# A gated delta rule's z products and gates, moved from behind the four groups into each group

## The chip, the cores and the metric

The kernel runs on one core of a Trainium2 chip, in one launch. The metric is device microseconds of one execution. Three runs of the kernel before took 2798.03, 2798.21 and 2803.38 us; the median is 2798.21.

The engines are named as in the profile: PE is TensorE (matmul and transpose; PEld its weight loads), DVE is VectorE, ACT is ScalarE, POOL is GpSimd, SP is SyncE, which issues nearly all DMA transfers.

## The reference

Two blocks of two layers over 512 positions of width 1024, in float32. The change touches one mixer of the second block, the gated delta rule:

```
proj = x @ w_in                         # q, k, v, z of 8 heads x 128, and gates
q, k, v = silu(conv4(q, k, v))          # then q, k normalised per head
# per head, in chunks: A = strict_lower((beta k) k^T * decay); solve (I + A) u = beta v
for chunk n:                            # state S: 128 x 128 per head
    v_new = u_n - w_n S
    o_n   = (q_n * exp(gc)) S + (q k^T * decay) v_new
    S     = S * d_n + k_dec^T v_new
o = rms_norm(o, norm_w) * silu(z)       # z: the gate of the output
return o @ w_o                          # here gdn_wo
```

Behind it come residual, layer norm and a mixture of 16 experts, then a second layer.

## The kernel before

Every product with weights is done three times with float32r halves (`mm3`: high x high, high x low, low x high). A piece of weights, 128 x 1024, is loaded by SP (`ws<-in_...`, 512 KB), its high half copied out on ACT (L130), its low half formed on DVE (L131); `ws` has 4 buffers, the halves 3 each.

`gdn` (L786) works on four groups of two heads. `gdn_group` (L894) does in program order:
- products of k, q and v (`lin_f`, six pieces of gdn_w, 24 matmuls of 128x512 each), convolution and silu on DVE and ACT, transposes to token order (L917);
- decay and k q^T for four chunks of 128 positions, giving B and Q (L973 to L985);
- the inverse of I + A on its 16x16 diagonal blocks: B is stored to DRAM (L998), the diagonal blocks are loaded as W (L999), solved on DVE in small steps (L1002 to L1028), stored (L1029) and loaded back as X (L1030);
- transposes of X (L1034) and three levels that widen the inverse to 32, 64 and 128 (L1036 to L1069): matmuls L1055, L1062, L1065, then L1044 and L1049, each level with DVE steps between;
- the scan over the four chunks (L1075 to L1120), which leaves the output `ot` and its sums of squares; then the root (`rsqrt`, 12 small DVE steps).

Behind all four groups come the products of z (`lin_t`, L872): for each group two pieces of gdn_wz and, for four token tiles, 24 matmuls of 128x256; each result goes through tanh on ACT (L869) and one DVE step (L870) into `sz`. Then, per head, four gates on DVE (L884), four transposes (L885), a scaled copy on ACT (L886) and its low half on DVE (L887) give `ys`. `out_moe` (L1125) multiplies `ys` with gdn_wo in products of 24 matmuls; a product needs all eight heads, k by k.

Buffers are rings named by a tag: x has 16 buffers of 128 x 1024 (the input `xs` holds 8 until the last product with it, a group holds KQ twice, ktok and vtok), h has 4 (`ot`). In PSUM, `lin` has 2 banks, `s` 3, `o` 2, `pt` 1.

The code gives a program order. The order in each engine's queue is fixed when the program is built: instructions are taken in program order, but one whose inputs or buffer are not ready yet (by the builder's own reckoning) is overtaken by later ones that are. On the chip each queue then runs strictly in that order.

Of the kernel before, what the change touches and what calls it, by code (L numbers as in the profile page):

```python
# [11 lines left out]
AF = mybir.ActivationFunctionType  # L12
OP = mybir.AluOpType
# [7 lines left out]
NT = 4  # L21
# [8 lines left out]
def rd(ap):  # L30
    return ap.bitcast(F32)


class Kern:
# [751 lines left out]
    def gdn(self):  # L786
        nc, xs = self.nc, self.xs
# [6 lines left out]
        def ev_ab(o, p):  # L794
# [9 lines left out]
        a, e, u, v = (self.small((128, 2 * U), x) for x in ("a", "e", "u", "v"))  # L804
# [14 lines left out]
                                       op0=OP.mult, op1=OP.mult)  # L819
# [34 lines left out]
        for x in self.xdram:  # L854
            nc.sync.dma_start(x[:1024].rearrange("(p n) c -> p (n c)", p=128), zero)
            nc.sync.dma_start(x[1024:], zero[:8, :128])
        ot = []
        for grp in range(4):
            ot.append(self.gdn_group(grp))
            self.strips_skew(grp)  # L860
        hr = self.small((128, NT), "hr")
        nc.vector.tensor_scalar(hr, self.rcol, 0.5, None, op0=OP.mult)
        sz = []

        def ev_z(c, t, p):
            if t == 0:
                sz.append(self.T("sz", "x").rearrange("p (n i c) -> p n i c", n=NT, i=2))
            th, z = self.t("zt", tag="P")[:, :256], sz[c].rearrange("p n i c -> p n (i c)")[:, t]
            nc.scalar.activation(th, p, AF.Tanh, scale=hr[:, t:t + 1])  # L869
            nc.vector.scalar_tensor_tensor(z, th, 1.0, p, op0=OP.add, op1=OP.mult)  # L870

        self.lin_t(self.wap("gdn_wz", 8, 256), range(4), xs, ev_z)  # L872
        ys = self.ys = [self.rpair("gy") for _ in range(8)]
        for grp in range(4):
            o, rs = ot[grp]
            nc.vector.tensor_tensor(rs.rearrange("p (n i) -> p n i", i=2), rs.rearrange("p (n i) -> p n i", i=2),
                                    self.rcol[:, :, None].to_broadcast([128, NT, 2]), op=OP.mult)
            for i in range(2):
                h = 2 * grp + i
                p = self.psum("o")  # L880
                for n in range(NT):
                    u = 2 * n + i
                    ou = o[:, u * 128:(u + 1) * 128]
                    nc.vector.scalar_tensor_tensor(ou, ou, rs[:, u:u + 1], sz[grp][:, n, i], op0=OP.mult, op1=OP.mult)  # L884
                    nc.tensor.transpose(p[:, n * 128:(n + 1) * 128], ou, self.ident)  # L885
                nc.scalar.activation(ys[h][0], p, AF.Copy, scale=nw)  # L886
                nc.vector.scalar_tensor_tensor(ys[h][1], p, nw, rd(ys[h][0]), op0=OP.mult, op1=OP.subtract)  # L887
        self.dump_ys("d_gy", self.ys)
# [5 lines left out]
    def gdn_group(self, grp):  # L894
        nc, xs, wv, lvl = self.nc, self.xs, self.gconv, self.lvl
# [26 lines left out]
        ss = self.small((128, 16), "ss", tag="gA", bufs=3)  # L922
# [27 lines left out]
        g16 = lambda x: x.rearrange("p (n i) -> p n i", i=2)  # L950
# [22 lines left out]
        for n in range(NT):  # L973
# [4 lines left out]
            for i in range(2):  # L978
                u = 2 * n + i
# [11 lines left out]
        ublk = lambda x, u: x[:, u * 128:(u + 1) * 128]  # L991
# [36 lines left out]
            product(V, (0, 1), V, (0, 0), W, (1, 0))  # L1028
        nc.sync.dma_start(diag(xd), rc(V))  # L1029
        nc.sync.dma_start(v8(X), full(xd))  # L1030
        for hf in range(2):
            p = self.psum("s")
            for j in range(4):
                nc.tensor.transpose(p[:, j * 128:(j + 1) * 128], ublk(X, 4 * hf + j), self.ident)  # L1034
            self.copy(Y[:, hf * S:(hf + 1) * S], p)
# [36 lines left out]
        ot = self.T("ot", "h")  # L1072
        ss = self.small((128, 8), "oss", tag="gss", bufs=4)
# [45 lines left out]
            if n < NT - 1:  # L1119
                Sp = Sn  # L1120
        nc.vector.tensor_scalar(ss, ss, 1.0 / 128, 1e-6, op0=OP.mult, op1=OP.add)
        return ot, self.rsqrt(ss, 8)


    def out_moe(self, wname, ys, layer, out=None):  # L1125
# [917 lines left out]
```

## Time and profile before

| | |
|---|---|
| median of the runs | 2798.21 us |
| profiled execution | 2798.65 us, span 2796.9 us |
| PE busy | 2682.8 us (96%) |
| DVE busy | 1770.3 us (63%) |
| ACT busy | 1367.6 us (49%) |
| POOL busy | 181.9 us (7%) |
| DMA | 332.58 MB, mean 119 GB/s |
| mean granted clock of TensorE | 0.982 |

The delta rule lies between about 1505 and 1850 us of the span. Busy shares are averages over stages with different limits; the rows below show this stage by itself.

### The profile page before, as it was taken

The numbers are of one execution on the slowest core, as the hardware profiler recorded it, in microseconds if no ns is written. First come the engines' busy times: TensorE is split into PE (matmuls) and PEld (weight loads), VectorE is DVE, ScalarE is ACT, GpSimd is POOL, SyncE is SP. The second block draws the span as 40 slices with busy tenths as digits, with TensorE's granted clock in tenths as the row PEclk, the third lists the DMA queues.
The fourth block names the chain that finished last, engine by engine and source line by source line (L and its number), as shares of the span: only waits on it lengthen the run. The fifth ranks groups of instructions, "written<-read, shape, count | busy, mean of one in ns | idle before, by whom it ended". The sixth has DMA issues, their size and how long they took to land. (4 is left out here: it accounts for less than half of the span.)

```text
span 2796.9 us, 40163 instructions
## 1 busy us (share of the span) xinstructions
PE 2682.8 (96%) x15128; PEld 2294.2 (82%) x15128; DVE 1770.3 (63%) x3583; ACT 1367.6 (49%) x2541; POOL 181.9 (7%) x185
## 2 busy tenths in 40 slices
PE   8999999999999999999999999997997999997996
PEld 6889888888888888888887788997886888897885
DVE  6775564443447656535445877567878367667878
ACT  5654443332346544423334644335885255534885
POOL 1101010000111010100002000000001001000001
PEclk9999999999999999999999999998999999998998
DMA  4314233333333331334433222323887212013985
GB/s 138 100 41 148 70 94 92 97 98 98 91 86 92 106 106 42 109 98 127 149 94 128 85 71 63 93 69 129 303 291 275 91 42 73 24 45 100 313 295 190
DMA packets 122534, 332.58 MB, mean 119 GB/s; under 512 B 21716, under 2 KB 37748, under 8 KB 122328
## 3 DMA queue, kind: packets, MB, share of 16 engines
q1 hardware_dynamic: 119896, 321.43, 36.4%
q0 software_dynamic: 2432, 8.46, 0.8%
q8 instruction: 123, 2.02, 0.3%
q14 instruction: 83, 0.68, 0.1%
HBM read 301.49 MB, written 28.02 MB: 118 GB/s over the span
## 5 line engine op out<-in xcount | busy, mean ns | idle before, releaser
L130 ACT ACTIVATE wh<-ws 128x1024 fp32r<-128x1024 f32 (+2 forms) x521 | 534.1, 1030 | 828.8 <-PE lin L153 594.8
L131 DVE TENSOR_TENSOR wl<-ws,wh 128x1024 fp32r<-128x1024 f32 (+2 forms) x521 | 616.6, 1192 | 154.8 <-ACT wh L130 152.5
L152 PE MATMUL lin<-xs,wh 128*128 128x512 f32 (+2 forms) x1080 | 428.3, 397 | 7.4 <-ACT xs L197 5.9
L153 PE MATMUL lin<-xs,wh 128*128 128x512 f32 (+2 forms) x1080 | 429.0, 397 | 2.6 <-DVE xs L198 2.4
L154 PE MATMUL lin<-xs,wl 128*128 128x512 f32 (+2 forms) x1080 | 427.7, 396 | 0.9 <-DVE wl L131 0.9
L152 PEld LDWEIGHTS lin<-xs,wh 128*128 128x128 f32 (+2 forms) x1080 | 202.9, 188 | 50.9 <-ACT xs L197 6.8
L153 PEld LDWEIGHTS lin<-xs,wh 128*128 128x128 f32 (+2 forms) x1080 | 203.0, 188 | 47.6 <-DVE xs L198 7.1
L154 PEld LDWEIGHTS lin<-xs,wl 128*128 128x128 f32 (+2 forms) x1080 | 203.0, 188 | 42.3 <-DVE wl L131 1.4
L347 DVE TENSOR_TENSOR h<-lin,h 128x512 f32<-128x512 f32 x112 | 77.4, 691 | 247.6 <-PE lin L154 247.5
L152 PE MATMUL lin<-sr,wh 128*128 128x512 f32 x512 | 199.2, 389 | 0.0
L153 PE MATMUL lin<-sr,wh 128*128 128x512 f32 x512 | 199.2, 389 | 0.0
L154 PE MATMUL lin<-sr,wl 128*128 128x512 f32 x512 | 199.2, 389 | 0.0
L734 DVE SCALAR_TENSOR_TENSOR ra<-lin,bc 128x512 f32<-128x512 f32 x64 | 44.3, 692 | 168.5 <-PE lin L154 165.9
L305 ACT ACTIVATE P<-s,mn 128x256 f32<-128x256 f32 (+1 forms) x224 | 114.3, 514 | 52.7 <-DVE mn L303 50.1
L1539 PE MATMUL o<-oh,Rh 128*128 128x256 f32 x512 | 131.1, 292 | 5.6 <-PEq L1382 2.2
L1539 PE MATMUL o<-oh,Rl 128*128 128x256 f32 x512 | 130.0, 290 | 0.0
L152 PEld LDWEIGHTS lin<-sr,wh 128*128 128x128 f32 x512 | 96.1, 188 | 20.1
L154 PEld LDWEIGHTS lin<-sr,wl 128*128 128x128 f32 x512 | 96.1, 188 | 19.9
L153 PEld LDWEIGHTS lin<-sr,wh 128*128 128x128 f32 x512 | 96.1, 188 | 19.8
L153 PE MATMUL s<-wl,exh 128*128 128x512 f32 x256 | 105.1, 410 | 5.3 <-DVE wl L131 5.1
L313 PE MATMUL o<-c_ident,P 128*128 128x128 f32 x536 | 97.0, 282 | 12.2 <-ACT P L305 11.4
L1539 PEld LDWEIGHTS o<-oh,Rh 128*128 128x128 f32 x512 | 101.7, 199 | 8.6 <-ACT ex L1555 4.1
(605 smaller groups left out, 6174.4 us busy)
## 6 DMA issues: line engine op xcount, KB each, us to landing
ws<-in_moe_wgu SPq DMA_DIRECT2D x128, 512.0 KB, 5.9
ws<-in_mlp_wu SPq DMA_DIRECT2D x64, 512.0 KB, 3.6
ws<-in_mlp_wd SPq DMA_DIRECT2D x64, 512.0 KB, 3.6
ws<-in_moe_wd SPq DMA_DIRECT2D x64, 512.0 KB, 5.6
yd<-ey SPq DMA_DIRECT2D x56, 256.0 KB, 4.7
ws<-in_gdn_w SPq DMA_DIRECT2D x24, 512.0 KB, 3.7
ws<-in_ab_w SPq DMA_DIRECT2D x16, 512.0 KB, 4.4
ws<-in_xa_wk SPq DMA_DIRECT2D x16, 512.0 KB, 3.7
```

Of the source, the lines that this page charges most:

```text
L130: nc.scalar.activation(wh, ws, AF.Copy)
L131: nc.vector.tensor_tensor(wl, ws, rd(wh), op=OP.subtract)
L152: mm(out, a[0], b[0], start=start, stop=False)
L153: mm(out, a[0], b[1], start=False, stop=False)
L154: mm(out, a[1], b[0], start=False, stop=stop)
L305: nc.scalar.activation(P[:, :nk], p[:, :nk], AF.Exp, bias=mn, scale=-1.0, accum_out=den)
L313: nc.tensor.transpose(pt[:, b * 128:(b + 1) * 128], P[:, b * 128:(b + 1) * 128], self.ident)
L347: self.nc.vector.tensor_tensor(self.hT[n], p, self.hT[n], op=OP.add)
L734: nc.vector.scalar_tensor_tensor(a, p, 0.0, rms()[1], op0=OP.max, op1=OP.mult)
L1539: self.nc.tensor.matmul(p[:, j * 256:(j + 1) * 256], Rs[t][i][:, fs], oh[:, t], start=t + i == 0, stop=t == NT - 1 and i == 1)
```

## The change

The products of z and their evacuation move from `gdn` into `gdn_group`, behind the load of X and ahead of its transposes; each group makes only its own `sz`. The factor of the root and the eight gates of a group move to the end of `gdn_group`, which returns the gated `ot`. The half of `rcol` (`hr`) is formed ahead of the groups. What is left behind the groups is transposes, scaling and splitting. No matmul, transfer or other step is added or taken away.

```diff
+        self.hr = self.small((128, NT), "hr")
+        nc.vector.tensor_scalar(self.hr, self.rcol, 0.5, None, op0=OP.mult)
         ot = []
         for grp in range(4):
             ot.append(self.gdn_group(grp))
             self.strips_skew(grp)
-        hr = self.small((128, NT), "hr")
-        nc.vector.tensor_scalar(hr, self.rcol, 0.5, None, op0=OP.mult)
-        sz = []
-
-        def ev_z(c, t, p):
-            if t == 0:
-                sz.append(self.T("sz", "x").rearrange("p (n i c) -> p n i c", n=NT, i=2))
-            th, z = self.t("zt", tag="P")[:, :256], sz[c].rearrange("p n i c -> p n (i c)")[:, t]
-            nc.scalar.activation(th, p, AF.Tanh, scale=hr[:, t:t + 1])
-            nc.vector.scalar_tensor_tensor(z, th, 1.0, p, op0=OP.add, op1=OP.mult)
-
-        self.lin_t(self.wap("gdn_wz", 8, 256), range(4), xs, ev_z)
         ys = self.ys = [self.rpair("gy") for _ in range(8)]
         for grp in range(4):
-            o, rs = ot[grp]
-            nc.vector.tensor_tensor(rs.rearrange("p (n i) -> p n i", i=2), rs.rearrange("p (n i) -> p n i", i=2),
-                                    self.rcol[:, :, None].to_broadcast([128, NT, 2]), op=OP.mult)
             for i in range(2):
                 h = 2 * grp + i
                 p = self.psum("o")
                 for n in range(NT):
                     u = 2 * n + i
-                    ou = o[:, u * 128:(u + 1) * 128]
-                    nc.vector.scalar_tensor_tensor(ou, ou, rs[:, u:u + 1], sz[grp][:, n, i], op0=OP.mult, op1=OP.mult)
-                    nc.tensor.transpose(p[:, n * 128:(n + 1) * 128], ou, self.ident)
+                    nc.tensor.transpose(p[:, n * 128:(n + 1) * 128], ot[grp][:, u * 128:(u + 1) * 128], self.ident)
...
         nc.sync.dma_start(diag(xd), rc(V))
         nc.sync.dma_start(v8(X), full(xd))
+
+        sz = self.T("sz", "x")
+
+        def ev_z(c, t, p):
+            th, z = self.t("zt", tag="P")[:, :256], sz[:, t * 256:(t + 1) * 256]
+            nc.scalar.activation(th, p, AF.Tanh, scale=self.hr[:, t:t + 1])
+            nc.vector.scalar_tensor_tensor(z, th, 1.0, p, op0=OP.add, op1=OP.mult)
+
+        self.lin_t(self.wap("gdn_wz", 8, 256), [grp], xs, ev_z)
         for hf in range(2):
...
-        return ot, self.rsqrt(ss, 8)
+        rs = self.rsqrt(ss, 8)
+        nc.vector.tensor_tensor(g16(rs), g16(rs), self.rcol[:, :, None].to_broadcast([128, NT, 2]), op=OP.mult)
+        for u in range(8):
+            ou = ublk(ot, u)
+            nc.vector.scalar_tensor_tensor(ou, ou, rs[:, u:u + 1], ublk(sz, u), op0=OP.mult, op1=OP.mult)
+        return ot
```

## Rows read from the trace of the kernel before

**Rows 1.** Busy time by stretch (us; busy and instructions by engine, clock, DMA share, GB/s).
```profile
1573.40:1636.20 62.80, 61.95 (x385) 52.55 (x384) 46.67 (x94) 29.02 (x82) 1.84 (x2) 1.00 0.25 70
1636.20:1699.40 63.20, 60.83 (x392) 52.05 (x391) 47.75 (x114) 31.76 (x92) 1.84 (x2) 1.00 0.21 61
1699.40:1764.20 64.80, 63.42 (x422) 55.20 (x421) 49.80 (x117) 31.09 (x92) 1.84 (x2) 1.00 0.23 68
1764.20:1849.80 85.60, 81.61 (x655) 79.94 (x654) 55.27 (x155) 32.55 (x73) 0.40 (x4) 0.94 0.33 101
```
**Rows 2.** Timeline of SyncE's issues (start, us, queue, line, transfer, count).
```profile
1580.12 3.42 SPq L129 DMA_DIRECT2D ws<-in_gdn_w  x2
...
1661.80 0.33 SPq L129 DMA_DIRECT2D ws<-in_gdn_w  x1
1672.68 0.33 SPq L129 DMA_DIRECT2D ws<-in_gdn_wz  x1
...
1764.19 0.38 SPq L998 DMA_DIRECT2D b<-B  x1
```
**Rows 3.** Timeline of TensorE where the products of z begin (start, us).
```profile
1741.40 0.48 PE L154 MATMUL lin<-xs,wl 128*128 128x512 f32 x1
1741.71 0.28 PE L152 MATMUL lin<-wh,xs 128*128 128x256 f32 x1
1741.83 0.28 PE L153 MATMUL lin<-wl,xs 128*128 128x256 f32 x1
```
**Rows 4.** Busy time of line L152 alone, ahead of group 3's store (PE, PEld).
```profile
1741.60:1764.20 22.60, 3.76 (x13) 2.33 (x13) 1.00 0.08 24
```
**Rows 5.** Timeline of TensorE, first transposes and products with gdn_wo.
```profile
1836.61 1.04 PE L885 MATMUL o<-c_ident,ot 128*128 128x128 f32 x8
...
1838.86 0.39 PE L152 MATMUL lin<-wh,gy 128*128 128x256 f32 x1 [1.06 <-ACT gy L886]
...
1849.80 0.28 PE L154 MATMUL lin<-wh,gy 128*128 128x256 f32 x1
```
**Rows 6.** Timeline of TensorE, levels of groups 0 and 1 (idle before, releaser).
```profile
1601.42 1.07 PE L1034 MATMUL s<-c_ident,X 128*128 128x128 f32 x8 [0.45 <-DMA X<-x]
...
1665.41 1.09 PE L1034 MATMUL s<-c_ident,X 128*128 128x128 f32 x8 [1.83 <-DMA X<-x]
...
1667.76 0.39 PE L917 MATMUL pt<-c_ident,KQ 128*128 128x128 f32 x2
...
1687.19 0.36 PE L980 MATMUL s<-gmask,identr 128*128 128x256 f32 x1
...
1687.62 0.61 PE L1092 MATMUL o<-vtok,X 128*128 128x128 f32 x4
```
**Rows 7.** Timeline of TensorE, levels of group 3.
```profile
1787.97 1.09 PE L1034 MATMUL s<-c_ident,X 128*128 128x128 f32 x8 [2.40 <-DMA X<-x]
1790.27 3.51 PE L1055 MATMUL s<-Y,B 128*128 128x64 f32 x16
...
1800.39 2.00 PE L1055 MATMUL s<-Y,B 128*128 128x64 f32 x16
...
1812.19 0.61 PE L1092 MATMUL o<-vtok,X 128*128 128x128 f32 x4
```
**Rows 8.** Busy time by stretch of 2 us, with the granted clock.
```profile
1790.00:1792.00 2.00, 2.00 (x12) 2.00 (x11) 1.19 (x2) 0.00 (x0) 0.00 (x0) 0.50 0.19 14
...
1796.00:1798.00 2.00, 2.00 (x19) 2.00 (x19) 0.00 (x0) 0.00 (x0) 0.00 (x0) 0.96 0.56 227
```
**Rows 9.** Busy time by stretch of 10 us, the routing behind.
```profile
1910.00:1920.00 10.00, 7.53 (x38) 7.46 (x39) 6.38 (x38) 2.07 (x5) 0.00 (x0) 0.55 0.01 4
1920.00:1930.00 10.00, 5.40 (x40) 4.92 (x40) 5.66 (x24) 4.41 (x8) 0.15 (x1) 0.96 0.53 157
```
**Rows 10.** Timeline of VectorE, root and last gates of group 3.
```profile
1832.69 0.17 DVE L1121 TENSOR_SCALAR oss<-oss 128x8 f32<-128x8 f32 x1 [0.82 <-ACT jk L1118]
...
1835.53 1.67 DVE L884 SCALAR_TENSOR_TENSOR ot<-ot,b,sz 128x128 f32<-128x128 f32 x6
...
1838.69 0.62 DVE L884 SCALAR_TENSOR_TENSOR ot<-ot,b,sz 128x128 f32<-128x128 f32 x2
```
**Rows 11.** Instructions of four source lines: ns min/median/max, first and last start.
```profile
L870 DVE SCALAR_TENSOR_TENSOR sz<-zt,lin x16: 401/415/422, 1765.6 to 1838.2; 128x256 f32<-128x256 f32 x16
L884 DVE SCALAR_TENSOR_TENSOR ot<-ot,b,sz x32: 222/346/352, 1766.0 to 1839.0; 128x128 f32<-128x128 f32 x32
L886 ACT ACTIVATE gy<-o,gdn_nw x8: 678/689/692, 1838.1 to 1847.7; 128x512 fp32r<-128x512 f32 x8
L887 DVE SCALAR_TENSOR_TENSOR gy<-o,gdn_nw,gy x8: 743/749/753, 1839.2 to 1848.4; 128x512 fp32r<-128x512 f32 x8
```

## The prediction, made before the changed kernel was built or run

> **What bounds the kernel now.** I read the page's busy table first, then busy time by stretch for the delta rule, then the timelines of SyncE, TensorE and VectorE around its end. TensorE is the engine that is full: between one group's store of B and the next one's it idles 0.85, 2.37 and 1.38 us in periods of 62.8, 63.2 and 64.8 us, while VectorE has 15 to 16 us free in each [rows 1]. So in groups 0 to 2 the kernel is bound by the sum of TensorE's work, and the long chain of a group (store of B, inverse, transfer back, levels, scan) is covered by products of others.
>
> What covers it is to be seen in the order of the queues. Loads of the next group's weights stand between the store of B and the transfer back of group 0; the gate's weights are first loaded right after the last of the 24 pieces of gdn_w [rows 2], and the first product of z starts 0.31 us after the last product of group 3 [rows 3]. The order is thus the program's, except that what waits for something is overtaken by later work that is ready. Group 3 has no next group. Its cover is z: in the 22.6 us ahead of its store of B, 13 matmuls of L152, so some 39 of the 384 for z, are issued [rows 4]; the other 345 at 0.12 us each [rows 3], 41 us, lie beside group 3's chain, and TensorE is busy 81.61 of the 85.6 us from that store to the end of the first two products with gdn_wo [rows 1, 5].
>
> **The change part by part.** *The products of z.* Each group gets its own 96 matmuls (8 slices of k, 3 products, 4 token tiles), 96 x 0.12 = 11.5 us [rows 3]. They stand in program order ahead of the transposes of X and ahead of the next group's products, and their two loads of 512 KB ahead of the next group's loads. "Behind the inverses' transfer" does not hold them there: a load that is ready overtakes a waiting transfer, as those of gdn_w did [rows 2]. Total work is the same, so the question is only what each piece now covers. Groups 0 to 2 have their cover already, and the new products delay everything behind them: group 3's store of B comes 3 x 11.5 = 34.6 us later, less what falls into idle time. That idle is 0.85 + 2.37 + 1.38 = 4.6 us at most [rows 1], much of it waits for the transfer of X in an ordered queue (0.45 and 1.83 us, [rows 6]) that stay; I take 1.5 us back. Ahead of group 3's store the place of the 39 matmuls of now is taken by its own z. **First term: +33 us** (bounds +30 to +35; +40 with a bubble, the third rival).
>
> *Group 3's chain without its cover.* From the store of B to the end of the second product with gdn_wo it takes 85.6 us now [rows 1, 2, 5]. Piece by piece, now and after:
> - store to transposes of X: 1764.19 to 1787.97, 23.8 us. Mostly transfers and VectorE; the rest of group 3's z (under 60 matmuls, 7 us) lies here. 23 (21 to 24).
> - levels, to the scan's first product: 1787.97 to 1812.19, 24.2 us [rows 7]; in group 1, at full clock and with products between, 22.2 [rows 6]. Without products between, at most 2 us less; but TensorE will have stood for long. Now, after 2.4 us of waiting, the granted clock went to 0.50, its lower level of 1.2 GHz, until about 1796 [rows 7, 8], and the same 16 matmuls of L1055 took 3.51 us there and 2.00 at 2.4 GHz [rows 7]. All six such groups slow would be 9 us. In 1910 to 1920, with TensorE 75% busy, the clock was 0.55, in the next stretch 0.96 at 54% [rows 9]. So half of that: 25 (20 to 30).
> - scan: 1812.19 to 1832.69, 20.5 us [rows 7, 10]; half a us less for each of four steps without z between, some of it lost again to the clock. 20 (18 to 24).
> - root and gates: 1832.69 to 1835.53 for the root, then eight gates at 1.67 / 6 = 0.28 us [rows 10]; the eight need no longer wait for z's last tile, as the last two do now (1838.69). 5 (to 6.6 now).
> - transposes, scaling and split to the end of two products: until 1849.80 now, 10.5 us after the last gate's end at 1839.3. In the new kernel heads 0 to 5 are gated long before, so their transposes and 36 of the 48 matmuls of each pair of products are done in the chain's idle time. Left are 2.25 us from transpose to first product [rows 5], under 1 us for the second head (estimate from 0.69 and 0.75 us for a scaling and a split, [rows 11]) and 12 matmuls at 0.12: 4.5 (4 to 6).
>
> Sum 77.5 against 85.6: **second term -8 us** (-18 to +3). **Third term +1 us** (0 to +3): the remaining products with gdn_wo start at the lower clock where they now start at 1.0 or nearly.
>
> The Trainium skill, "TensorE: Matmul & The Clock Gate", section "Part 1: The HAM clock gate", has the throttled state as the default, released only by activity. By that rule alone the levels and the scan of a bare chain run slow throughout, and the sum would be about 9 us more than mine; the rows just named show both levels at such shares, and I go by them.
>
> *The gates at each group's end.* 32 gates of 0.346 us and 16 evacuations of 0.415 us on VectorE [rows 11] move forward: per group 8 x 0.35 + 4 x 0.42 = 4.4 us, and two splits of weights, into periods with 15 us free there [rows 1]. They cost nothing on the path, except behind a split that TensorE waits for; at most some 2 us a group if that cover were gone (estimate: half of it), inside the bounds. The tanh on ScalarE moves with them; hr moves as one small instruction. Zero.
>
> **Sum.** +33 - 8 + 1 = +26 us. On the profiled execution's 2798.65 us (span 2796.9) that is 2824.6; against the median of the runs, 2798.21, 2824. As a check by work: of those 77.5 us TensorE has about 38 of work, so 39 stand idle, against 4 idle and 5 lost to the clock now [rows 1]: +30, less the idle filled before.
>
> **The rivals.**
> - *The fill moves for nothing, no change.* Group 2's last k and q were transposed at 1667.76 and its decay products began only at 1687.19 [rows 6]: 20 us of slack. If that slack carries the delay of z(0) and z(1), group 3's store moves by some 20 us only, and with a chain at full clock (-18) the sum is +2: 2801. Against it: TensorE has no idle time for the displaced work to go to.
> - *The other sign: the order keeps z late.* If the products of z are held back (by a buffer of the ring, by weights) and group 3 keeps them as cover, the first two terms vanish and the gain at the end stays: 10.5 - 4.5 = 6 us, and 1.5 of idle: 2791. It decides when most of z is still undone at the last store of B. For it: z's results need a buffer that group 3's predecessors hold. Against: only two banks of PSUM take products, so a held z also stops the next group's.
> - *A bubble from buffers.* The ring x has 16 buffers; the layer's input takes 8, a group 5 instead of 4, so two groups no longer fit, and v of the next group and its z wait for the scan. At some 4 us in groups 1 to 3: +38, 2837. TensorE's idle time per period would show it.
>
> The Trainium skill, "Perfetto Trace Analysis", section "Optimization Strategy", reads a gap that repeats on the engine that should be full as a sign that buffers ran out. The trace of before shows no such gap beyond the transfer of X; the rule would lend this last rival its place.
>
> **How the numbers follow.** Forecast 0.62, no change 0.12, z kept late 0.13, bubble 0.13. The likeliest's own range is 2811 to 2843 by the ends of the terms; the range given, 2796 to 2838, leaves out most of the z-late case and the top of the bubble. Under 0.2% (5.6 us) a measurement of this kernel can't tell from none: faster 0.13, same 0.11 (most of the no-change case), slower 0.76.
>
> **What would show it.** The loads of gdn_wz four times two, between the pieces of gdn_w, not after them. Period from store to store near 74 us, or 63 with a growing backlog; group 3's store of B near 1797. From there to the first complete product with gdn_wo 70 to 85 us, TensorE idle for some 35 us of it, with clock near 0.5 in parts. Wrong if TensorE stays above 90% busy in that stretch (then z was kept late), or if the store comes before 1785.

## The result, and the profile after

The changed kernel takes 2843.55 us (median of four runs, 2838.25 to 2849.26) against 2798.12 us for the kernel before (2796.59 to 2803.38): ratio 1.0167, interval 1.0149 to 1.0186. The forecast was 2824 with a range to 2838: the sign was right, the loss of 45 us was forecast as 26. The profiled execution of the changed kernel was its shortest, 2838.25 us, so the two profiles differ by 39.6 us only; its longer runs had lower mean granted clocks (0.973, 0.971, 0.969; 0.975 in the profile).

The page's busy time of TensorE and its count of instructions, changed kernel:

```profile
PE 2697.7 (95%) x15128; PEld 2306.1 (81%) x15128; DVE 1773.9 (63%) x3583; ACT 1368.3 (48%) x2541; POOL 183.3 (6%) x185
```

It is 14.9 us more for as many instructions (2682.8 us and x15128 before): the same work, part of it at a lower clock.

Busy time by stretch, changed kernel (columns as in [rows 1]): the three periods from one group's store of B to the next one's, then the 85.9 us from group 3's store to the end of the first two products with gdn_wo.

```profile
1570.10:1644.10 74.00, 72.38 (x473) 62.74 (x472) 54.33 (x121) 35.82 (x97) 1.84 (x2) 1.00 0.25 70
1644.10:1728.30 84.20, 81.61 (x534) 71.64 (x534) 61.06 (x144) 36.34 (x99) 1.84 (x2) 0.98 0.24 68
1728.30:1802.70 74.40, 72.55 (x474) 62.94 (x474) 54.29 (x121) 35.76 (x97) 1.84 (x2) 1.00 0.23 70
1802.70:1888.60 85.90, 59.76 (x353) 54.21 (x352) 35.61 (x100) 18.56 (x44) 0.40 (x4) 0.72 0.21 66
```

Against [rows 1] each period is longer by 9 to 21 us of TensorE's work (the middle one holds 126 matmuls of z, the others 64 and 66), with 1.62, 2.59 and 1.85 us idle for 0.85, 2.37 and 1.38. In the last row TensorE is busy 59.76 us for 81.61, the clock is 0.72 for 0.94, and the stretch is as long as before. SyncE's issues show that z now stands among the groups, and when the chain starts (answers to [rows 2]):

```profile
1514.75 0.36 SPq L129 DMA_DIRECT2D ws<-in_gdn_wz  x1
...
1577.06 6.61 SPq L129 DMA_DIRECT2D ws<-in_gdn_wz  x2
...
1802.72 0.38 SPq L983 DMA_DIRECT2D b<-B  x1
```

Group 0's store of B is issued at 1570.09. Its own weights for z are loaded 48 to 55 us ahead of it (1514.75, the second piece at 1522.33); the two loads right behind it and ahead of the load of X (1588.14) are those of group 1. "Behind the load of X" thus holds in program order only: of a group's 96 matmuls of z, 63, 31, 61 and 31 (groups 0 to 3) run ahead of their own group's store, the others right behind it. Group 3's store is issued at 1802.72, 38.5 us later than at 1764.19. What its chain then does, TensorE's levels (answers to [rows 7]) and the clock in stretches of 5 us (busy time, clock, DMA share, GB/s):

```profile
1824.73 1.94 PE L1028 MATMUL s<-c_ident,X 128*128 128x128 f32 x8 [14.02 <-DMA X<-x]
1826.56 3.67 PE L1049 MATMUL s<-Y,B 128*128 128x64 f32 x16
...
1839.01 3.68 PE L1049 MATMUL s<-Y,B 128*128 128x64 f32 x16 [0.83 <-DVE Y L1061]
...
1856.79 1.23 PE L1086 MATMUL o<-vtok,X 128*128 128x128 f32 x4 [0.77 <-DVE X L1045]
```

```profile
1803.00:1808.00 5.00, 5.00 (x44) 1.00 0.46 136
...
1818.00:1823.00 5.00, 0.00 (x0) 0.50 0.28 63
...
1838.00:1843.00 5.00, 3.86 (x17) 0.50 0.36 108
...
1863.00:1868.00 5.00, 3.15 (x22) 0.98 0.00 0
```

TensorE waits 14 us for X, the granted clock falls to 0.50 (1.2 GHz), and all six groups of 16 matmuls of 128x64 in the levels run there: 3.62 to 3.68 us each where the second L1055 of [rows 7] took 2.00. Only in the scan does the clock come back.

### The profile page after: what moved, and what is told of

It is laid out like the page before. It is cut to its first block, busy times and chain, and to the rows that moved or that the text cites. A ratio compares the mean times of both kernels' runs of the same rounds, so it can differ in the third digit from the quotient of the medians.

```text
span 2836.5 us, 40183 instructions
## 1 busy us (share of the span) xinstructions
PE 2697.7 (95%) x15128; PEld 2306.1 (81%) x15128; DVE 1773.9 (63%) x3583; ACT 1368.3 (48%) x2541; POOL 183.3 (6%) x185
## 5 line engine op out<-in xcount | busy, mean ns | idle before, releaser
L152 PE MATMUL lin<-xs,wh 128*128 128x512 f32 (+2 forms) x1080 | 428.5, 397 | 7.3 <-ACT xs L197 5.8
L152 PEld LDWEIGHTS lin<-xs,wh 128*128 128x128 f32 (+2 forms) x1080 | 202.6, 188 | 50.1 <-ACT xs L197 7.0
L152 PE MATMUL lin<-sr,wh 128*128 128x512 f32 x512 | 199.2, 389 | 0.0
L153 PEld LDWEIGHTS lin<-sr,wh 128*128 128x128 f32 x512 | 96.1, 188 | 19.9
L152 PEld LDWEIGHTS lin<-sr,wh 128*128 128x128 f32 x512 | 96.1, 188 | 19.9
```

Source lines behind the costliest of these rows:

```text
L152: mm(out, a[0], b[0], start=start, stop=False)
L153: mm(out, a[0], b[1], start=False, stop=False)
```

## The experiments

In the table, "loss" is (ratio - 1) x 2797 us; "store" is the issue of group 3's store of B in the profiled run; "X to scan's end" runs from the transposes of X to VectorE's first step behind the scan (the end stands in no row below: it is the last start of that step, 1832.69 in [rows 10]).

| kernel | median us | ratio (interval) | loss | store | X to scan's end |
|---|---|---|---|---|---|
| before | 2798.1 | 1 | 0 | 1764.2 | 44.7 |
| changed | 2843.6 | 1.0167 (1.0149-1.0186) | 46.7 | 1802.7 | 53.5 |
| e5 changed, no z of groups 0-2 | 2809.0 | 1.0046 (1.0032-1.0060) | 12.9 | 1763.2 | 56.1 |
| e6 before, no z of groups 0-2 | 2805.4 | 1.0032 (1.0020-1.0045) | 9.0 | 1761.9 | 58.4 |
| e1 useless z behind | 2834.8 | 1.0129 (1.0102-1.0156) | 36.1 | 1800.4 | 43.3 |
| e9 z of groups 1-3 behind | 2804.6 | 1.0028 (1.0015-1.0041) | 7.8 | 1778.8 | 41.1 |
| e2 z of groups 2-3 behind | 2831.6 | 1.0113 (1.0086-1.0139) | 31.6 | 1789.7 | 54.5 |
| e8 z of group 3 behind | 2845.2 | 1.0176 (1.0158-1.0195) | 49.2 | 1803.4 | 58.4 |
| e3 gates behind | 2845.2 | 1.0165 (1.0143-1.0187) | 46.2 | 1805.1 | 58.4 |
| e4 ys in another tag | 2834.7 | 1.0138 (1.0115-1.0161) | 38.6 | 1801.7 | 53.6 |
| e10 filling, z of group 3 pushed back | 2837.1 | 1.0138 (1.0113-1.0164) | 38.6 | 1802.6 | 53.6 |
| e11 half of that filling | 2841.4 | 1.0163 (1.0133-1.0192) | 45.6 | 1801.4 | 53.9 |
| e13 filling behind X | 2830.2 | 1.0121 (1.0102-1.0140) | 33.8 | 1805.8 | 43.3 |
| e14 e13 and e4 | 2827.4 | 1.0109 (1.0092-1.0126) | 30.5 | 1802.0 | 42.8 |
| e12 e9 and e4 | 2802.0 | 1.0018 (1.0006-1.0029) | 5.0 | 1776.4 | 42.3 |
| e7 before, ys early | 2795.4 | 0.9986 (0.9977-0.9995) | -3.9 | 1765.0 | 44.6 |

Theory: z was free cover beside group 3's chain and is now on the path ahead of it, and the bare chain runs at the lower clock. Rivals: the ring x runs out of buffers; the gates hold up VectorE; the bare chain is bound by latencies, not by the clock.

**The same work left out of both kernels.** In `gdn_group` (e5) and in `gdn` (e6) the z products of groups 0 to 2 give way to `nc.gpsimd.memset(sz, 1.0)`. The edit of e5:

```diff
-        self.lin_t(self.wap("gdn_wz", 8, 256), [grp], xs, ev_z)
+        if grp < 3:
+            nc.gpsimd.memset(sz, 1.0)
+        else:
+            self.lin_t(self.wap("gdn_wz", 8, 256), [grp], xs, ev_z)
```

> The changed kernel, leaving out the z products of groups 0 to 2 (288 matmuls of about 0.12 us, 34.6 us; the gate's factor of those groups is set to one). Theory (these products lie on the path ahead of group 3's store of B): the time falls by all of them and by the idle around them, 34 to 42 us below the changed kernel (2801 to 2810). Rival (the loss is in the loads' buffers or in the gates, which stay): falls by less than 25 us.

> The kernel before, leaving out the z products of groups 0 to 2 (the same 288 matmuls; the gate's factor of those groups is set to one). Theory (behind the groups they were cover for group 3's chain, free): the time falls by 0 to 8 us only (2790 to 2798), the chain then runs bare, its levels at a clock of 0.50 to 0.7. Rival (their work is worth the same wherever it stands): falls by 28 to 38 us (2760 to 2770).

In the changed kernel these 34.6 us of TensorE work are worth 46.7 - 12.9 = 33.8 us: they are on the path. (Between the two profiled runs the store moves by 39.5 us, of which e5's chain, 7.0 us longer from the store to the scan's end, hides a part; what makes it longer is left open.) In the kernel before, leaving them out makes it 9.0 us slower, beyond what I expected: they were not only free there, the chain needed them. TensorE in e6, the levels, and the clock in stretches of 5 us:

```profile
1785.61 1.97 PE L1038 MATMUL s<-c_ident,X 128*128 128x128 f32 x8 [13.24 <-DMA X<-x]
1787.47 3.68 PE L1059 MATMUL s<-Y,B 128*128 128x64 f32 x16
```

```profile
1797.00:1802.00 5.00, 4.16 (x20) 0.50 0.30 105
...
1817.00:1822.00 5.00, 3.30 (x12) 0.50 0.03 11
...
1837.00:1842.00 5.00, 4.43 (x18) 0.50 0.00 0
```

The clock is 0.50 through levels and scan, the first of them 3.68 us for 16 matmuls, and the scan ends 11.3 us later than before, from a store issued 2.3 us earlier. So the loss of 46.7 us splits, in this order of steps, into 9.0 for the lost cover (before to e6), 3.9 for the rest of the change (e6 to e5; the two intervals overlap, so it may be nothing), and 33.8 for z on the path (e5 to the changed kernel).

**Cover that is useful to nobody.** Behind the groups:

```diff
+        self.lin_t(self.wap("gdn_wz", 8, 256), range(3), xs, ev_again)   # a tanh into scratch
```

> The changed kernel, with the z products of groups 0 to 2 done a second time behind the groups, as filling only (their results go through a tanh into a scratch tile and are dropped): 288 matmuls of about 0.12 us, 34.6 us of TensorE work that nobody needs. Theory (cover): group 3's dependent chain ran bare at a granted clock of 0.50 in its levels; with other products between its steps the clock stays near 0.95, the levels fall from 32.1 to 22 to 26 us and the run is 4 to 10 us faster than the changed kernel (2833 to 2839). Rival (the bare chain is bound by the latency from engine to engine, not by the clock): same time within 2 us, or slower by what the filling queues in front of the chain, up to +10.

34.6 us of work more, and 8.8 us less by the medians (10.6 by the ratios, whose intervals just overlap); from X to the scan's end 43.3 us for 53.5, of which the levels take 22.8 for 32.1. So the latencies from engine to engine, which are the same, are not what makes the bare chain 53.5 us long. The clock in the levels of e1:

```profile
1820.00:1825.00 5.00, 3.19 (x20) 0.81 0.81 233
...
1830.00:1835.00 5.00, 5.00 (x46) 1.00 0.19 55
```

**How many groups' z stand behind.** `if grp not in (2, 3)` and the like ahead of the z products of a group; those left out, with their gates, come behind the groups as before.

> The changed kernel, with z and gates of groups 1 to 3 behind the groups as before, only group 0's in its group. Cover theory: 96 matmuls, 11.5 us, ahead of the store, 34.6 us of cover left: +6 to +14 (2804 to 2812). Rival (the z of group 0 falls into idle time of the first group, and the cover left is enough): +0 to +4.

> The changed kernel, with the z products of groups 2 and 3, and their gates, behind the groups as before, those of groups 0 and 1 in their groups. Cover theory: some 192 matmuls stand ahead of group 3's store of B instead of 314, of which 22 us are new on the path, and group 3's chain keeps 23 us of cover: +15 to +25 over the kernel before (2813 to 2823), about half of the change's loss. Rival (buffers of ring x, five more per group, make the loss): the rings are as full in groups 0 and 1, so well over half of the loss stays only if those two hold the bubble, and a bubble of group 2 alone (84 us period) goes: +26 to +30. Rival (gates at a group's end make the loss): gates of two groups gone, +20 to +25.

> The changed kernel, with z and gates of group 3 alone behind the groups as before, those of groups 0 to 2 in their groups. Cover theory: 288 of 314 matmuls still stand ahead of group 3's store; 11.5 us of cover: 2828 to 2840 (+30 to +42). Rival (latency-bound chain, cover worth nothing but its own work): 2840 to 2844 less the 3 us of z of group 3 ahead of the store.

e9 came as the theory said; e2 lost more (31.6 us for 15 to 25), close to what the ring's buffers as the cause would give (26 to 30), but TensorE's idle time in its three periods (1.7, 2.3 and 2.4 us) shows no bubble; e8 lost as much as the changed kernel (49.2 for 30 to 42). The loss doesn't grow in proportion: with three, two, one and no group's z left behind the groups it is 7.8, 31.6, 49.2 and 46.7. The store comes 14.6, 25.5, 39.2 and 38.5 us later; what jumps is the time from X to the scan's end, 3.6 us shorter than before in e9 and 9.8 longer in e2. TensorE in e2 shows why: its z filled the wait for X and was used up there.

```profile
1813.35 1.09 PE L1044 MATMUL s<-c_ident,X 128*128 128x128 f32 x8 [1.51 <-DMA X<-x]
1814.76 2.00 PE L1065 MATMUL s<-Y,B 128*128 128x64 f32 x16 [0.31 <-ACT Y L782]
...
1823.78 3.68 PE L1065 MATMUL s<-Y,B 128*128 128x64 f32 x16 [0.83 <-DVE Y L1077]
```

The first level starts at 2.4 GHz (2.00 us), the second runs at 1.2 (3.68); the clock falls within the first level (0.56 from 1819 to 1824), with no longer wait than the 1.51 us for X and gaps of 0.3 to 0.9 us: here the gaps were enough. e9 waited as long for X, but one group more of z lasts through the levels, the clock is 1.00 (1804 to 1814 in the second fence), and X to scan's end takes 41.1 us.

```profile
1801.29 1.06 PE L1044 MATMUL s<-c_ident,X 128*128 128x128 f32 x8 [1.53 <-DMA X<-x]
```

```profile
1804.00:1809.00 5.00, 5.00 (x46) 1.00 0.57 161
1809.00:1814.00 5.00, 5.00 (x44) 1.00 0.69 262
```

**Filling that can't start before X.** In group 3, weights copied from X make 96 matmuls (e10), or 48 (e11), wait for it:

```diff
+            nc.scalar.activation(fz, X[:, :128], AF.Copy)            # fz: one buffer of wh
...
+                for k in range(24):
+                    nc.tensor.matmul(p, fz, xs[k % 8][0][:, :256], start=k == 0, stop=k == 23)
```

> The changed kernel with 96 useless matmuls of 128x256 (11.5 us at full clock) whose weights are a copy of X of group 3, so that none can start ahead of X's arrival: they stand between the steps of the levels and of most of the scan. Nothing fills the wait from the store of B to X, which stays idle. Theory (the half clock comes from a chain with gaps and goes back to full when the gaps are filled): some 5 us at 0.50 behind the idle wait, then 1.00; levels 23 to 27 us for 32.1, scan 20 for 21.5; 6 to 10 us faster than the changed kernel (2834 to 2838) with a third of the filling of the run with 288. Rival 1 (the idle wait ahead of the levels makes the half clock, whatever follows): levels stay at 0.50 and every filling matmul takes 0.21 us more in the chain: 5 to 15 us slower than the changed kernel. Rival 2 (it was the amount of work behind the store that counted): no difference within 2 us.

> As the run with 96 useless matmuls that wait for X, with 48 of them (5.8 us), which stand between the steps of the levels alone; the scan is bare. Theory: levels 23 to 27 us; the scan starts at full clock and keeps it or falls within it (20 to 24 us); 4 to 9 us faster than the changed kernel (2835 to 2840). Rival 1 (idle wait makes the half clock): levels at 0.50 and slower by 2 to 8 us. Rival 2 (amount counts): same within 2 us.

Both totals mislead: the copy stood in program order ahead of z of group 3, so the splits of its weights waited on ScalarE, z came behind X, and 13.6 us passed from the last transposes of X (1823.56) to the first level (1837.14). The levels themselves took 19.0 us in e10 (to 1856.15) for 30.2 in the changed kernel (1826.56 to 1856.79), but the matmuls of z just ahead of them had brought the clock to 1.00 already, so these two runs don't show what the filling does. What e11 does show: its scan, bare again, kept the clock at 1.00 and took 19.9 us. A stretch of it:

```profile
1858.00:1863.00 5.00, 2.98 (x20) 1.00 0.69 219
```

In e13 the copy stands behind z:

> As the run with 96 useless matmuls that wait for X, with their weights' copy behind the z products of group 3 in the program: in that run the copy stood on ScalarE ahead of the split of these z products' weights, so that z of group 3 came behind X and into the chain (13.6 us between the transposes of X and the first level). Theory (gaps in the chain make the half clock; filling gives it back): a few us at 0.50 behind the idle wait, then 1.00; from the transposes of X to the end of the scan 44 to 47 us for 53.5; 5 to 9 us faster than the changed kernel (2834 to 2839). Rival (amount of work behind the store counts, or the idle wait holds the clock down): within 2 us of the changed kernel or slower.

```profile
1825.45 1.94 PE L1032 MATMUL s<-c_ident,X 128*128 128x128 f32 x8 [14.01 <-DMA X<-x]
...
1836.32 1.99 PE L1053 MATMUL s<-Y,B 128*128 128x64 f32 x16
```

The clock in e13, in stretches of 5 us:

```profile
1822.00:1827.00 5.00, 1.55 (x8) 0.50 0.35 105
1827.00:1832.00 5.00, 5.00 (x34) 0.73 0.49 153
1832.00:1837.00 5.00, 5.00 (x46) 1.00 0.80 276
...
1862.00:1867.00 5.00, 4.12 (x20) 0.68 0.34 107
```

The same 14 us of waiting take the clock to 0.50, but it is back at 1.00 by 1832, the second level's L1053 (1836.32) takes 1.99 us, the levels take 22.5 us for 32.1, and from X to the scan's end it is 43.3 us. 12.9 us of the loss are gone (46.7 - 33.8; 9.8 between the profiled runs, 5 to 9 expected), with a third of e1's filling. So the wait ahead of X takes the clock down, but neither that wait nor the amount of work behind the store keeps it down through the levels: what stands between the steps decides. When the filling had run out, late in the scan, the clock fell again (0.68). A bare scan can do either, as e11 shows; what decides there is left open.

**The gates.** The gates of all groups back behind the groups:

```diff
-            nc.vector.scalar_tensor_tensor(ou, ou, rs[:, u:u + 1], ublk(sz, u), op0=OP.mult, op1=OP.mult)
-        return ot
+        return ot, rs, sz                      # gated ahead of each transpose of ys
```

> The changed kernel, z products within their groups, with the gates of all groups moved back behind the groups. Cover theory: VectorE and ScalarE have idle time in the groups, the gates cost there nothing; the end gets 0 to 3 us longer by gates of heads 0 to 5 that crowd behind the root: within -2 to +4 us of the changed kernel. Rival (the gates stand in VectorE's queue ahead of the next group's splits and hold the store of B): 5 to 12 us faster than the changed kernel.

46.2 us of loss for 46.7, and the store comes no earlier (1805.1 for 1802.7), as it would if the gates held it: they cost nothing that can be seen where they are.

**ys held by a ring.** `p = self.psum("s")` for `psum("o")` at the transposes of ys.

> The changed kernel, with the transposes of ys in the PSUM tiles of another tag than those of the scan. Theory (the tiles of one tag are handed out in program order, so the ys of heads 0 to 5, gated long before, stood behind the scan's last tile): they now run in the idle time of group 3's chain, the end behind the scan gets 2 to 6 us shorter: 2838 to 2842. Rival (they were held by PE's own queue order, or the end is set by heads 6 and 7 alone): same within 1.5 us.

> The same filling, and the transposes of ys in PSUM tiles of another tag than the scan's. The two repair different parts of the lost cover (the clock of levels and scan; the ys of heads 0 to 5 behind the scan), so their gains should add up: 3 to 6 us faster than the run with the filling alone, 2828 to 2835; what is left over the kernel before is then the first term, z on the path, 33 to 38 us. Rival (the ys in the idle wait already gave the clock back, so the two are one gain): within 1.5 us of the run with the filling alone.

> The z products and gates of group 0 alone in its group, those of groups 1 to 3 behind the groups, and the transposes of ys in PSUM tiles of another tag than the scan's. Against the run with group 0's z early (2804.6 us, ratio 1.0028 to the kernel before): theory (ys held by the order of the tag's tiles) 2 to 6 us shorter at the end, so 0.9975 to 1.0015 of the kernel before. Rival (with z cover behind, the ys have no idle time to fill, or sit in front of z in the queue): ratio stays at 1.002 to 1.005.

The line of these transposes, first in the changed kernel, then in e4 (ns min/median/max, first and last start):

```profile
L870 PE MATMUL o<-c_ident,ot x32: 270/273/329, 1874.9 to 1886.5; 128*128 128x128 f32 x32
```

```profile
L870 PE MATMUL s<-c_ident,ot x32: 271/418/476, 1854.9 to 1882.2; 128*128 128x128 f32 x32
```

With tiles of another tag they start 20 us earlier. In the changed kernel they came only among the scan's last products, as they must if the buffers of a tag are handed out in program order. Tag "s" is that of the levels, and in e4 the ys start right behind the levels' last product (1853.05), so even there the wait for X stays empty. The gain is 8.1 us by the ratios, 4.5 between the profiled runs; on top of e13 3.3, on top of e9 2.8. The intervals are 3 to 7 us wide to a side, and none of these gains is clear of them by itself: that the ys were held is shown, what it cost (3 to 8 us) is not settled. Part of it may be clock: in e4 it is at 0.92 from 1858 to 1863, with the ys and their products in the scan, where the changed kernel still had 0.50. By the medians e4 gained more than I expected, e14's loss of 30.5 is below the 33 to 38 forecast, and e12 ended just above the band I gave it.

**A version below both.** The kernel before, with the gates of groups 0 to 2 between its z products, and the ys of heads 0 to 5 in tiles "s" ahead of the last two z tiles of group 3:

```diff
+        w3 = list(wz(3))
+        for t in range(2):
+            self.lin_1(w3, t, xs, lambda p: ev_z(3, t, p))
+        for grp in range(3):
+            turn(grp)                          # transposes and splits of its ys
+        for t in range(2, NT):
+            self.lin_1(w3, t, xs, lambda p: ev_z(3, t, p))
```

> The kernel before, with the transposes and splits of ys of heads 0 to 5 in PSUM tiles of another tag and ahead of the last two z tiles of group 3, so that only heads 6 and 7 stand behind the root. Theory (behind the chain's end the kernel before does 48 ys matmuls on the path, of which 36 needn't be there): 2 to 5 us faster than before (2793 to 2796). Rival (the gates of heads 0 to 5 are not done by then, and their ys stand ahead of the last z tiles in TensorE's queue): same within 1 us, or slower by up to 4.

0.9986 (0.9977 to 0.9995): 3.9 us faster than the kernel before, in the band. It keeps z where it was.

## Why the prediction came out too low

Of the 39.6 us between the profiles I had forecast 26: the first term was 5.5 us short, the second 8.3, the third 0.2 too large. The other 5.8 us between forecast and median loss (45.4) lie between the profiled run and the median of the four, and stay open.

- *What bounds the kernel, and that z is cover:* right, and more so than I wrote. By e6 the cover is worth 9 us beyond its own work.
- *First term, +33:* the mechanism was right (e5: 33.8 us for the z products), the term too small: 38.5 us between the stores. I took 1.5 us of idle back; instead the three periods idle 1.5 us more. The period of 84.2 us holds a wait for X (2.0 us) and a clock of 0.98 (1.7 us lost, an estimate from 84.2 x 0.02), and by group 3's store all of group 2's scan is done, of which some 2 us came behind that store before.
- *Second term, -8:* failed; 85.9 us for 85.6. The step that failed is the levels: "half of that: 25 (20 to 30)". They took 32.1 us, all six groups slow. I had weighed the clock by [rows 9], a stretch of other work, and halved the price; the whole price was due, and e1 and e13, where the same levels took 22.8 and 22.5 us, show that it was the clock's. Store to X took 22.0 us (23 forecast), the scan 21.5 (20), root and gates 7.1 (5), the rest 3.2 (4.5).
- *Heads 0 to 5 done in the chain's idle time:* failed. No ys was transposed ahead of 1874.9; four of their splits then stood on VectorE within the root, which took 5.0 us for the 2.84 of [rows 10]. I had looked at when the inputs are ready, not at which ring the tiles come from.
- *Third term, +1:* 39.6 - 38.5 - 0.3 = 0.8 by the profiles. The number came out by luck, its reason did not: behind the first two products with gdn_wo the clock is 1.00 in both kernels (1849.8 to 1855 before, 1888.6 to 1894 after). It was the kernel before that ran the first of them at the lower clock:

```profile
1839.00:1844.00 5.00, 4.48 (x24) 0.66 0.49 151
```

- *Gates at nothing:* right as far as e3 can tell.
- *The rivals:* "no change" and "z kept late" are out by the stores. The bubble's figure, 2837, is nearest to the profiled 2838.25, but its sign, 4 us of idle in each of groups 1 to 3, isn't there (1.62, 2.59 and 1.85).
- *Signs:* store at 1802.7 for about 1797, periods of 74.0, 84.2 and 74.4 for 74, 85.9 us to the products with gdn_wo for 70 to 85. TensorE stood idle for 26.1 us of it, not some 35: at the lower clock the same work fills more of the time.
- *Range:* too narrow above. The levels' own bound, 30, was too low, and the top was cut at 2838. The 2843 that I gave as the likeliest's end doesn't follow from its terms: 35 + 3 + 3 = 41 us end at 2839, and the pieces of the second term, whose upper ends add up to 90.6 us and so +5, at 2841.

The rule that I set aside, in the Trainium skill, "TensorE: Matmul & The Clock Gate", section "Part 1: The HAM clock gate", says that the array is throttled unless activity releases it. It would have added 9 us; the levels came 7.1 over my figure. For the scan the trace goes only half with it: in the changed kernel the clock was 0.98 and more from 1863, in e11 1.00 throughout, in e6 0.50 to the scan's end.

Left open: what makes the changed kernel's other runs up to 11 us longer than its profiled one. Bare chains took 53.5 to 58.4 us in the table, so a chain that gets its clock back later would explain about half; those runs have no profile.

## What to carry to other kernels

Work that stands beside a dependent chain is cover: moving it ahead of the chain cost nearly all of it here (by e5, 33.8 of 34.6 us), and the chain, left bare, may lose clock on top. Count how long the cover lasts: here the first 22 us of it go into the transfer's wait, and only what is left over reaches the steps that it keeps fast. To let finished results run early, look at the tag of their tiles: they come behind whatever earlier work takes its tiles from the same tag. A tag that no part of the chain uses was not tried.

## What the hardware showed that I had not expected

Useless matmuls made the changed kernel faster: 96 of them (11.5 us of work) took 12.9 us off. And the same bare scan ran at either level: at 1.00 in e11's 1858 to 1863 (2.98 us busy in 5) and at 0.98 in the changed kernel's 1863 to 1868 (3.15), at 0.50 in e6's 1817 to 1822 (3.30, with 12 matmuls where the changed kernel's stretch holds 22). So the busy share of a stretch did not tell its clock.
